# Other places for the results of the odd down projections, the mixer's weights kept as two parts, and GpSimd's tensor_tensor moved to VectorE

## The chip, the cores and the metric

The kernel runs on one core of one Trainium2 chip. The metric is the device time of one execution in microseconds (us); lower is better. Inputs and outputs lie in the chip's DRAM and are float32.

## What is computed

One layer of a streaming encoder on 2048 tokens of width 1024. The parts that matter here:

```python
mix = token_mixer(rms_norm(h, pre_mix_g), w_in, ..., w_out)   # p = xn @ w_in, mixing, y @ w_out
h = h + rms_norm(mix, post_mix_g)
f = rms_norm(h, pre_ffn_g) @ w_up                             # 1024 -> 2 x 2816
f = causal_dwconv3(f, ffn_conv_w) + ffn_conv_b
gate, up = split(f, 2)
ffn = (gelu(gate) * up) @ w_down                              # 2816 -> 1024
h = h + rms_norm(ffn, post_ffn_g)
```

The token mixer projects with `w_in`, has a gated short convolution over 512 channels and eight heads of a state recurrence (chunks of 64 tokens), and maps back with `w_out`.

## The kernel before

**Layout.** Channels lie on the 128 partitions, tokens along the free axis, in four token blocks of 512 (`TB`). Every matmul operand in full precision is split in two parts, a rounded higher part (`hi`, a copy on ScalarE) and the rest (`lo`, a subtraction on VectorE), and each product is three matmuls: hi x hi, hi x lo, lo x hi. `split` does this. In `gemm` weights come in blocks of four 128 x 128 tiles (256 KB): a DMA into `wraw`, the split into `whi` and `wlo`, then 12 matmuls. Each of the three rings has three buffers.

**Stages.** First the mixer runs over blocks 0 to 3. In block 0 the scale of the input norm comes late (`late`), so that projections are multiplied by it behind the matmul; `short_conv` does two such multiplications on GpSimd. The weights `w_in` of 26 column tiles are the same in every block: `gemm` with a name in `keep` stores the `lo` part in DRAM when a block is first used, and blocks 1 to 3 load the raw weights, copy `hi` on ScalarE, and load `lo`. In block 0 the second half of each tile's `lo` is computed on GpSimd. `out_proj(b)` does the output projection with `w_out`, eight column tiles of two weight blocks each, all split anew for every token block; `residual(b)` adds the input. `out_proj` and `residual` of a block run beside the mixer of the next.

Then the channel mixer. `up(0)` does the up projection for token blocks 0 and 1 together, then `down_block(0)` and `down_block(1)` the down projection, then `up(1)`, `down_block(2)` and `down_block(3)`. `up` runs over 22 column pairs; in each, seven products of 12 matmuls (a Strassen-like scheme for two token blocks and two halves of the columns) with weights a11, s1, s2, a12, s3, s4, a22 and the operands b11, t1, t2, b21, t3, b22, t4 in this order. `up(0)` computes the four sums s1 to s4 (`summed`; s1 and s3 on GpSimd, s2 and s4 on VectorE) and stores them; `up(1)` loads them. Behind the products come the convolution (`cv`), the gate (`gt`) and a store.

**Places.** `slot(n)` numbers SBUF places of 2 KB per partition: 0 to 39 and 56 to 78 in one pool, 40 to 55 in those of the mixer's operands. The operands of `up` occupy places 0 to 55 in the order of the products, four slices of two parts each, so that t4 takes 48 to 55. `down_block` keeps its 22 operands in other places, by turns (`places`), and its eight results `fo` in 48 to 55:

```python
fo = [slot(48 + d, f"fo{b}_{d}", F32) for d in range(KT)]
```

`down` accumulates 66 matmuls into one of two PSUM banks (`psD`); ScalarE squares it for the norm and copies it to `fo`. `finish` computes the norm's scale, spreads it over the partitions with `over_partitions` (`ps` in PSUM, `rb` its copy in SBUF), and for each of the eight tiles loads the residual into one of two buffers `ho`, multiplies `fo` by the scale, adds into `ho` and stores:

```python
if d < 3:
    pool_e.tensor_tensor(out=fd, in0=fd, in1=rb, op=ALU.mult)
else:
    dve.tensor_tensor(out=fd, in0=fd, in1=rps, op=ALU.mult)
(pool_e if d < 2 else dve).tensor_tensor(out=hk, in0=fd, in1=hk, op=ALU.add)
```

In the last block `finish` runs twice, on half the tokens each, with residuals loaded ahead (`held`). The raw operands of a down projection pass through the ring `gk` of three buffers.

**Order.** All operations are recorded in a `Plan` first. It computes an order by list scheduling, with costs for each engine and operation (`cost`), delays between engines, ranks (`R_CHAIN` before `R_EVAC`, `R_PREP`, `R_OPERAND`, `R_WEIGHT`, `R_GEMM`) in the first round and the latest starts in 15 more, and issues all engines' instructions in the best order found (`emit`, line 431, which is why every row of the profile names L431). There is one plan for the mixer and one for the rest. Every DMA is issued from SyncE's queue. An engine works off its instructions in the order issued.

## Time and profile before

| | |
|---|---|
| time before, median of 3 runs | 2590.94 us (2590.84 to 2595.94) |
| the profiled execution's own time | 2591.45 us |
| its span, first to last instruction | 2589.7 us |
| mean granted TensorE clock | 0.986 of full speed |
| busy: TensorE, VectorE, ScalarE, GpSimd | 2479.0, 2025.0, 1476.6, 152.8 us |
| DMA | 432.29 MB, mean 167 GB/s |

PE is TensorE, PEld its weight load, DVE is VectorE, ACT ScalarE, POOL GpSimd, SP SyncE. Rows of groups give the line, the engine, the operation, output <- inputs by tile name, the shape, the count, then the busy time in us and the mean duration of one in ns, then the engine's idle time before them and what ended it. Matmuls overlap, so that the mean of a matmul (some 390 ns) is longer than the distance between two.

### The profile page before, as it was taken

How to read it: one execution, taken by the hardware profiler on the slowest of the kernel's cores; microseconds unless marked ns; L12 is line 12 of the kernel's file. 1: busy time of each engine (PE TensorE's matmuls, PEld its weight loads, DVE VectorE, ACT ScalarE, POOL GpSimd, SP SyncE). 2: the span in 40 equal slices, each digit the busy share in tenths (PEclk: the TensorE clock that was granted, in tenths of full speed). 3: DMA queues.
4: the chain of work that ended last, by engine and by line, in shares of the span. 5: the costliest groups of instructions: out<-in, count | busy, mean ns of one | idle time of the engine just before them, and what ended most of it. 6: DMA issues, size and time to landing. Idle time of an engine off the chain costs nothing.

```text
span 2589.7 us, 41292 instructions
## 1 busy us (share of the span) xinstructions
PE 2479.0 (96%) x14210; PEld 1948.8 (75%) x14210; DVE 2025.0 (78%) x4159; ACT 1476.6 (57%) x3070; POOL 152.8 (6%) x116
## 2 busy tenths in 40 slices
PE   8988999999999899989999999999989999999997
PEld 6766777777786677667877778788868888888886
DVE  7989878889786889768999999855478787784534
ACT  7555766566656555456656566543456666673532
POOL 1311000000000000001111121001010000000001
PEclk9999999999999899989999999999999999999998
DMA  6535454557454675465464634775654444454653
GB/s 204 175 100 167 130 172 131 165 163 257 130 171 148 203 248 163 150 202 179 154 192 147 202 131 167 249 247 172 190 183 126 122 118 130 120 160 130 191 183 106
DMA packets 239970, 432.29 MB, mean 167 GB/s; under 512 B 26640, under 2 KB 33424, under 8 KB 239760
## 3 DMA queue, kind: packets, MB, share of 16 engines
q1 hardware_dynamic: 239760, 429.65, 52.7%
q8 instruction: 112, 1.84, 0.3%
q14 instruction: 98, 0.80, 0.1%
HBM read 321.54 MB, written 108.00 MB: 166 GB/s over the span
## 4 chain that ended last, share of the span: by engine, by line
PE 64%; DVE 20%; DMA 8%; issue 4%; ACT 4%; SPq 0%; POOL 0%; DVEq 0%; ACTq 0%; POOLq 0%
PE dn L431 17%; PE upa L431 13%; PE upc L431 6%; PE op L431 5%; PE upb L431 3%; PE rp_ps L431 3%; PE kp_ps L431 2%; PE pc L431 2%; DVE cv L431 2%; PE vp_ps L431 2%; PE ch_ps L431 2%; PE cb_ps L431 1%; PE cc_ps L431 1%; DVE gt L431 1%; PE y L431 1%
## 5 line engine op out<-in xcount | busy, mean ns | idle before, releaser
L431 DVE TENSOR_TENSOR wd_l<-wd_r,wd_h 128x512 fp32r<-128x512 f32 x198 | 129.9, 658 | 200.0 <-ACT wd_h L431 190.9
L431 DVE SCALAR_TENSOR_TENSOR cv<-co,vec,cv 128x512 f32<-128x512 f32 x352 | 272.9, 800 | 13.5 <-ACT cv L431 12.1
L431 PE MATMUL dn<-gh,wd_h 128*128 128x512 f32 (+1 forms) x726 | 281.2, 388 | 0.9 <-ACT gh L431 0.6
L431 PE MATMUL dn<-gh,wd_l 128*128 128x512 f32 (+1 forms) x726 | 280.1, 386 | 0.2 <-DVE wd_l L431 0.2
L431 PE MATMUL dn<-gl,wd_h 128*128 128x512 f32 (+1 forms) x726 | 279.0, 384 | 0.2 <-DVE gl L431 0.2
L431 ACT ACTIVATE wd_h<-wd_r 128x512 fp32r<-128x512 f32 x198 | 117.4, 595 | 251.7 <-PE dn L431 220.4
L431 DVE SCALAR_TENSOR_TENSOR gt<-gt,cv 128x512 f32<-128x512 f32 x264 | 177.5, 694 | 2.0 <-ACT gt L431 0.8
L431 ACT ACTIVATE cv<-co,vec 128x512 f32<-128x512 f32 x176 | 142.3, 811 | 44.2 <-DVE co L431 35.4
L431 PEld LDWEIGHTS dn<-gl,wd_h 128*128 128x128 f32 x726 | 136.3, 188 | 30.2 <-DVE gl L431 1.3
L431 PEld LDWEIGHTS dn<-gh,wd_l 128*128 128x128 f32 x726 | 136.4, 188 | 30.0 <-DVE wd_l L431 0.4
L431 PEld LDWEIGHTS dn<-gh,wd_h 128*128 128x128 f32 x726 | 136.4, 188 | 29.3 <-ACT gh L431 1.7
L431 ACT ACTIVATE wua_h<-wua 128x512 fp32r<-128x512 f32 x132 | 82.6, 626 | 82.1 <-issue 38.4
L431 PE MATMUL op<-y_h,wo_h 128*128 128x512 f32 x256 | 101.6, 406 | 5.3 <-ACT y_h L431 4.2
L431 PE MATMUL op<-y_l,wo_h 128*128 128x512 f32 x256 | 102.4, 404 | 0.6 <-DVE y_l L431 0.4
L431 PE MATMUL op<-y_h,wo_l 128*128 128x512 f32 x256 | 101.7, 402 | 0.2
L431 DVE TENSOR_TENSOR wua_l<-wua,wua_h 128x512 fp32r<-128x512 f32 x132 | 96.9, 735 | 4.8 <-ACT wua_h L431 4.7
L431 ACT ACTIVATE wus_h<-wus 128x512 fp32r<-128x512 f32 x88 | 55.6, 632 | 68.2 <-PE upa L431 25.2
L431 DVE TENSOR_TENSOR ut<-nt,um 128x120 f32<-128x120 f32 (+24 forms) x248 | 70.0, 282 | 5.4
L431 DVE TENSOR_TENSOR um<-um,ut 128x120 f32<-128x120 f32 (+24 forms) x248 | 70.1, 283 | 5.2
L431 POOL TENSOR_TENSOR fo<-fo,fn_rb 128x512 f32<-128x512 f32 (+1 forms) x15 | 17.7, 1197 | 941.9 <-ACT fn_rb L431 941.9
L431 DVE TENSOR_TENSOR gl<-gk,gh 128x512 fp32r<-128x512 f32 x88 | 59.0, 687 | 16.1 <-ACT gh L431 15.9
L431 ACT ACTIVATE gt<-cv 128x512 f32<-128x512 f32 x88 | 55.0, 625 | 25.4 <-DVE cv L431 24.6
(731 smaller groups left out, 7081.0 us busy)
## 6 DMA issues: line engine op xcount, KB each, us to landing
wd_r<-in_w_down SPq DMA_DIRECT2D x165, 256.0 KB, 2.8
wua<-in_w_up SPq DMA_DIRECT2D x154, 256.0 KB, 3.0
g_d<-gt SPq DMA_DIRECT2D x88, 256.0 KB, 2.6
gk<-g_d SPq DMA_DIRECT2D x88, 256.0 KB, 3.3
wus<-s_d SPq DMA_DIRECT2D x88, 256.0 KB, 3.2
wo_r<-in_w_out SPq DMA_DIRECT2D x64, 256.0 KB, 3.3
s_d<-wu1s SPq DMA_DIRECT2D x44, 256.0 KB, 3.1
x<-in_x_t SPq DMA_DIRECT2D x32, 256.0 KB, 4.2
```

Source lines behind the costliest of these rows:

```text
L431: getattr(getattr(self.nc, e), m)(*[real(a) for a in args], **{k: real(a) for k, a in kw.items()})
```

## The change

It has four parts. (1) `down_block` of odd blocks (1 and 3) keeps its results 0 to 4 in places 51 to 55 and 5 to 7 in the ring `gk`; even blocks as before. (2) `gemm` with `keep` stores both parts of a weight block at its first use and loads both parts afterwards, without raw weights and without a split; `out_proj` uses it too. (3) Every tensor_tensor of GpSimd becomes VectorE's: the lower parts of kept weights in block 0, the late scale in `short_conv`, the sums s1 and s3, and the multiplications and additions of `finish`. (4) `finish` takes the scale from PSUM alone, and the copy `rb` falls away there. Since a plan orders everything, the order of all engines is computed anew.

```diff
--- before.py
+++ after.py
@@ -485,7 +485,13 @@
         act(hi, src, AF.Copy)
         lo_engine.tensor_tensor(out=lo, in0=src, in1=hi.bitcast(F32), op=ALU.subtract)
 
-    lower = {}
+    parts_d = {}
+
+    def store_parts(hi, lo, name):
+        there = [dram.tile([128, 4, 128], F32, name=f"{name}{p}") for p in "hl"]
+        for part, t in zip((hi, lo), there):
+            nc.sync.dma_start(out=t, in_=part.bitcast(F32))
+        return there
 
     def gemm(ps, src, nk, xs, name, keep=None, early=False):
 
@@ -495,19 +501,18 @@
         for k0 in range(0, nk, 4):
             n = min(4, nk - k0)
             plan.rank = R_PREP if early else R_WEIGHT
-            raw = wst.tile([128, 4, 128], F32, tag="wraw", name=f"{name}_r{k0}", bufs=WB[0])
-            nc.sync.dma_start(out=raw[:, 0:n, :], in_=src[:, k0:k0 + n, :])
             hi = wst.tile([128, 4, 128], F32R, tag="whi", name=f"{name}_h{k0}", bufs=WB[1])
             lo = wst.tile([128, 4, 128], F32R, tag="wlo", name=f"{name}_l{k0}", bufs=WB[1])
-            if (keep, k0) in lower:
-                act(hi, raw, AF.Copy)
-                nc.sync.dma_start(out=lo.bitcast(F32), in_=lower[keep, k0])
+            kept = parts_d.get((keep, k0))
+            if kept:
+                for part, there in zip((hi, lo), kept):
+                    nc.sync.dma_start(out=part.bitcast(F32), in_=there)
             else:
-                split(raw[:, 0:n, :], hi[:, 0:n, :], lo[:, 0:n, :],
-                      pool_e if keep and k0 else dve)
+                raw = wst.tile([128, 4, 128], F32, tag="wraw", name=f"{name}_r{k0}", bufs=WB[0])
+                nc.sync.dma_start(out=raw[:, 0:n, :], in_=src[:, k0:k0 + n, :])
+                split(raw[:, 0:n, :], hi[:, 0:n, :], lo[:, 0:n, :], dve)
                 if keep:
-                    lower[keep, k0] = dram.tile([128, 4, 128], F32, name=f"{keep}_l{k0}")
-                    nc.sync.dma_start(out=lower[keep, k0], in_=lo.bitcast(F32))
+                    parts_d[keep, k0] = store_parts(hi, lo, f"{keep}_{k0}")
             plan.rank = R_GEMM
             for k in range(n):
                 wh, wl = hi[:, k, :], lo[:, k, :]
@@ -541,7 +546,8 @@
                           op0=ALU.mult, op1=ALU.add)
         rsqrt(o1, ms, [128, n], name, out=out)
 
-    def over_partitions(y, name, pool, tag, bufs=1, both=False, n=4):
+    def over_partitions(y, name, pool, tag, bufs=1, n=4):
+
 
         dg = o1.tile([128, 4, 128], F32, tag="sq", name=f"{name}_dg")
         ps = psN.tile([128, TB], F32, tag="g", name=f"{name}_ps")
@@ -552,10 +558,12 @@
             for s in range(n):
                 nc.tensor.matmul(ps[:, s * 128:(s + 1) * 128], ones, dg[:, s, :],
                                  start=True, stop=True)
+        ps = ps[:, 0:n * 128]
+        if pool is None:
+            return ps
         rb = pool.tile([128, TB], F32, tag=tag, name=f"{name}_rb", bufs=bufs)[:, 0:n * 128]
-        ps = ps[:, 0:n * 128]
         act(rb, ps, AF.Copy)
-        return (rb, ps) if both else rb
+        return rb
 
     def token_sums(accs, name, n=4):
 
@@ -605,7 +613,7 @@
         acc = new_acc(f"oacc{b}")
         for d in range(KT):
             ps = psA.tile([128, TB], F32, tag="a", name=f"op{b}_{d}")
-            gemm(ps, w_out[d], KT, xs, f"wo{b}_{d}")
+            gemm(ps, w_out[d], KT, xs, f"wo{b}_{d}", f"wo{d}")
             ov = o1.tile([128, TB], F32, tag="ov", name=f"ov{b}_{d}", bufs=2)
             act(ov, ps, AF.Copy)
             nc.sync.dma_start(out=mix_d[b][:, d, :], in_=ov)
@@ -1159,8 +1167,8 @@
                 ps = proj(16 + 3 * j, f"cb{nm}")
                 dve.tensor_tensor(out=u[:, 2:TB + 2], in0=ps, in1=u[:, 2:TB + 2], op=ALU.mult)
                 if late is not None:
-                    pool_e.tensor_tensor(out=u[:, 2:TB + 2], in0=u[:, 2:TB + 2], in1=late,
-                                         op=ALU.mult)
+                    dve.tensor_tensor(out=u[:, 2:TB + 2], in0=u[:, 2:TB + 2], in1=late,
+                                      op=ALU.mult)
                 act(ucar[:, j, :], u[:, TB:TB + 2], AF.Copy)
                 cv = m1.tile([128, TB], F32, tag="cv", name=f"cv{nm}", bufs=1)
                 act(cv, u[:, 2:TB + 2], AF.Copy, scale=v_("conv_a", 8 + j))
@@ -1171,7 +1179,7 @@
                 ps = proj(17 + 3 * j, f"cc{nm}")
                 dve.tensor_tensor(out=cv, in0=ps, in1=cv, op=ALU.mult)
                 if late is not None:
-                    pool_e.tensor_tensor(out=cv, in0=cv, in1=late, op=ALU.mult)
+                    dve.tensor_tensor(out=cv, in0=cv, in1=late, op=ALU.mult)
                 nc.sync.dma_start(out=y_d[b][:, j, :], in_=cv)
 
             def first_operand():
@@ -1339,11 +1347,11 @@
                 split(raw, hi, lo, dve)
                 return hi, lo
 
-            def summed(a, b, op, j, engine, o=None):
+            def summed(a, b, op, j, o=None):
                 plan.rank = R_WEIGHT
                 if o is None:
                     o = next_slot(SUM, 2, f"wu{j}s{nm}", F32, (128, 4, 128))
-                engine.tensor_tensor(out=o, in0=a, in1=b, op=op)
+                dve.tensor_tensor(out=o, in0=a, in1=b, op=op)
                 nc.sync.dma_start(out=s_d[i][:, j, :, :], in_=o)
                 return o
 
@@ -1353,14 +1361,14 @@
                 a11, a12, a21, a22 = (load(x, n) for x, n in ((ga, "a11"), (gb, "a12"),
                                                               (ua, "a21"), (ub, "a22")))
                 yield parts(a11, "a11")
-                s1 = summed(a21, a22, ALU.add, 0, pool_e)
+                s1 = summed(a21, a22, ALU.add, 0)
                 yield parts(s1, "s1")
-                s2 = summed(s1, a11, ALU.subtract, 1, dve)
+                s2 = summed(s1, a11, ALU.subtract, 1)
                 yield parts(s2, "s2")
                 yield parts(a12, "a12")
-                s3 = summed(a11, a21, ALU.subtract, 2, pool_e)
+                s3 = summed(a11, a21, ALU.subtract, 2)
                 yield parts(s3, "s3")
-                s4 = summed(a12, s2, ALU.subtract, 3, dve, s2)
+                s4 = summed(a12, s2, ALU.subtract, 3, s2)
                 yield parts(s4, "s4")
                 yield parts(a22, "a22")
             else:
@@ -1485,7 +1493,9 @@
             if beside:
                 beside()
             plan.rank = R_EVAC
-            fo = [slot(48 + d, f"fo{b}_{d}", F32) for d in range(KT)]
+
+            fo = [f1.tile([128, TB], F32, tag="gk", name=f"fo{b}_{d}", bufs=3) if d > 4 and b % 2
+                  else slot((51 if b % 2 else 48) + d, f"fo{b}_{d}", F32) for d in range(KT)]
             acc = new_acc(f"facc{b}")
 
             def down(d, t, apart=False):
@@ -1504,19 +1514,16 @@
                 n = (t.stop - t.start) // 128
                 rf = f1.tile([128, 4], F32, tag="rf", name=f"rf{nm}")[:, 0:n]
                 inv_rms(token_sums(accs, nm, n), nm, rf, n)
-                rb, rps = over_partitions(rf, nm, o1, "nrb", both=True, n=n)
+                rps = over_partitions(rf, nm, None, "nrb", n=n)
                 for d in range(KT):
                     if last:
                         hk = held[d][:, t]
                     else:
-                        hk = f1.tile([128, TB], F32, tag="ho", name=f"ho{b}_{d}", bufs=2)
-                        nc.sync.dma_start(out=hk, in_=h_d[b][:, d, :])
+                        hk = f1.tile([128, TB], F32, tag="ho", name=f"ho{nm}_{d}", bufs=2)[:, t]
+                        nc.sync.dma_start(out=hk, in_=h_d[b][:, d, t])
                     fd = fo[d][:, t]
-                    if d < 3:
-                        pool_e.tensor_tensor(out=fd, in0=fd, in1=rb, op=ALU.mult)
-                    else:
-                        dve.tensor_tensor(out=fd, in0=fd, in1=rps, op=ALU.mult)
-                    (pool_e if d < 2 else dve).tensor_tensor(out=hk, in0=fd, in1=hk, op=ALU.add)
+                    dve.tensor_tensor(out=fd, in0=fd, in1=rps, op=ALU.mult)
+                    dve.tensor_tensor(out=hk, in0=fd, in1=hk, op=ALU.add)
                     nc.sync.dma_start(out=out_t[:, b, d, t], in_=hk)
 
             tokens = slice(0, TB)
@@ -1524,9 +1531,9 @@
                 down(d, tokens)
             if last:
 
-                held = [slot(d, f"ho{b}_{d}", F32) for d in range(KT)]
-                for d in range(KT):
-                    nc.sync.dma_start(out=held[d], in_=h_d[b][:, d, :])
+                held = [slot(d, f"ho{b}_{d}", F32) for d in range(KT if last else 0)]
+                for d, hk in enumerate(held):
+                    nc.sync.dma_start(out=hk, in_=h_d[b][:, d, :])
                 for t in (slice(0, TB // 2), slice(TB // 2, TB)):
                     plan.rank = R_EVAC
                     finish(t, [down(KT - 1, t, True), acc[:, t]])
```

## Rows read from the trace of the kernel before

**Rows 1.** Busy time by stretch: bounds, length, then each engine (x instructions), granted clock, DMA.
```profile
0.00:260.00 260.00, 227.03 (x1464) 171.32 (x1465) 230.29 (x504) 154.51 (x343) 49.82 (x46) 0.97 0.50 162
260.00:1180.00 920.00, 886.52 (x6751) 670.80 (x6750) 739.54 (x1956) 557.18 (x1264) 3.07 (x3) 0.98 0.55 175
1180.00:1626.00 446.00, 431.56 (x1865) 345.84 (x1864) 424.20 (x664) 278.71 (x567) 69.59 (x42) 0.99 0.50 166
...
1880.00:1936.00 56.00, 44.01 (x178) 32.13 (x177) 43.71 (x76) 28.69 (x53) 8.09 (x5) 0.91 0.61 195
1936.00:2323.00 387.00, 387.00 (x1690) 316.84 (x1689) 315.07 (x491) 246.14 (x472) 0.00 (x0) 1.00 0.45 128
2323.00:2590.00 267.00, 250.54 (x1166) 206.63 (x1164) 127.98 (x237) 100.64 (x178) 15.28 (x15) 0.97 0.51 154
sum 2590.00, PE 2479.01 PEld 1948.77 DVE 2025.03 ACT 1476.63 POOL 152.80; mean PE 354.14 PEld 278.40 DVE 289.29 ACT 210.95 POOL 21.83
```

**Rows 2.** The chain that ended last, longest pieces: start us, length us, what.
```profile
1649.07 110.16 PE dn L431 x479
...
1935.82 5.48 PE upa L431 x24
...
2301.38 5.56 PE upa L431 x24
```

**Rows 3.** Timeline of TensorE, second up pass: start, length, engine, [idle before <- releaser].
```profile
1880.62 0.39 PE L431 MATMUL upa<-b_10h,wua_h 128*128 128x512 f32 x1
...
1916.53 0.50 PE L431 MATMUL upa<-t_12h,wua_h 128*128 128x512 f32 x1 [3.35 <-ACT t_12h L431]
...
1923.09 0.80 PE L431 MATMUL upa<-t_13h,wua_h 128*128 128x512 f32 x1 [3.44 <-ACT t_13h L431]
```

**Rows 4.** Timeline of VectorE, GpSimd and ScalarE in the same step.
```profile
1891.33 0.68 DVE L431 TENSOR_TENSOR fo<-fo,fn_ps 128x512 f32<-128x512 f32 x1
...
1897.97 1.77 DVE L431 TENSOR_TENSOR b_13l<-xrb,b_13h 128x512 fp32r<-128x512 f32 x1
...
1908.20 1.32 DVE L431 TENSOR_TENSOR ho<-fo,ho 128x512 f32<-128x512 f32 x2
...
1921.68 1.40 DVE L431 TENSOR_TENSOR ho<-fo,ho 128x512 f32<-128x512 f32 x2 [3.30 <-DMA ho<-h_d]
...
1895.76 3.43 POOL L431 TENSOR_TENSOR ho<-fo,ho 128x512 f32<-128x512 f32 x2
...
1922.41 0.63 ACT L431 ACTIVATE t_13h<-xrt 128x512 fp32r<-128x512 f32 x1 [5.93 <-DVE ho L431]
```

**Rows 5.** Timeline of VectorE, from the first to the second down projection.
```profile
1779.80 0.69 DVE L431 TENSOR_TENSOR ho<-fo,ho 128x512 f32<-128x512 f32 x1 [0.80 <-DMA ho<-h_d]
```

**Rows 6.** Groups of VectorE in the first up pass, 1180 to 1620 us.
```profile
L431 DVE SCALAR_TENSOR_TENSOR cv<-co,vec,cv 128x512 f32<-128x512 f32 x166 | 139.0, 859 | 4.1 <-ACT cv L431 3.4
...
L431 DVE TENSOR_TENSOR wua_l<-wua,wua_h 128x512 fp32r<-128x512 f32 x64 | 50.0, 782 | 1.6 <-ACT wua_h L431 1.6
...
L431 DVE TENSOR_TENSOR wu1s<-wu0s,wua 128x512 f32<-128x512 f32 x21 | 14.3, 682 | 3.8 <-POOL wu0s L431 3.8
```

**Rows 7.** Groups of VectorE in the second up pass, 1940 to 2330 us.
```profile
L431 DVE SCALAR_TENSOR_TENSOR cv<-co,vec,cv 128x512 f32<-128x512 f32 x160 | 115.0, 748 | 8.3 <-ACT cv L431 7.6
...
L431 DVE TENSOR_TENSOR wua_l<-wua,wua_h 128x512 fp32r<-128x512 f32 x59 | 40.3, 684 | 0.0
```

**Rows 8.** Groups of ScalarE over the whole span.
```profile
L431 ACT ACTIVATE wo_h<-wo_r 128x512 fp32r<-128x512 f32 x64 | 39.8, 627 | 39.1 <-PE op L431 24.9 <-DMA wo_r<-in_w_out 6.6 <-DVE td L431 2.1
```

**Rows 9.** What TensorE waited for: us in total, times, longest us.
```profile
PE vp_ps L431 <- DMA vp_l<-wi_l: 1.3, 2, 0.8
```

**Rows 10.** Timeline of VectorE at the end of the last block.
```profile
2580.32 0.42 DVE L431 TENSOR_TENSOR fo<-fo,fn_ps 128x256 f32<-128x256 f32 x1 [1.18 <-PE fn_ps L431]
2581.27 0.42 DVE L431 TENSOR_TENSOR fo<-fo,fn_ps 128x256 f32<-128x256 f32 x1 [0.53 <-ACT fn_rb L431]
...
2584.63 1.63 DVE L431 TENSOR_TENSOR ho<-fo,ho 128x256 f32<-128x256 f32 x3
```

## The prediction

> **What bounds the kernel now.** I read the table of stretches first, one line per stage [rows 1]. TensorE is busy 2479 of 2590 us, so all that other engines can give back is some 111 us of its idle time, and the question of each edit is where in those it lies. The stages are the mixer of token block 0 (33.0 us idle), the mixers of blocks 1 to 3 with the output projection (33.5), the first pass of the up projection (14.4), the step from the second down projection into the second up pass (12.0 of 56) and the end of the last down projection (16.5 in the last line). Two stages run close to VectorE: 424.2 of 446 us in the first up pass, 230.3 of 260 in block 0. In the second up pass, without GpSimd, VectorE has 315 of 387 us and TensorE never waits. GpSimd works 152.8 us in all, 49.8 in block 0 and 69.6 in the first up pass.
>
> Then the chain that ended last, for the second up pass [rows 2]: the runs of 24 matmuls (last product of one column pair, first of the next) come every (2301.38 - 1935.82)/19 = 19.24 us. They are the last 20 of the 21 joins of 22 pairs, so the first joins pairs 1 and 2. The pass begins at 1880.62 [rows 3]. Unhindered, this join would start one pair and six of seven products later: 19.24 + 16.49 = 35.7 us, at 1916.4. It starts at 1935.82: 19.4 us lost, some 2 of them to the 16 small matmuls of the norm between. Of the other 17, 12.0 are idle [rows 1]; the rest are matmuls at the lower of the clock's two levels (granted 0.91 on average there against 1.00 later).
>
> Last, the timeline at that step. The long waits of TensorE are for the operand t4 [rows 3], which is written to places 48 to 55, and those hold the results `fo` of block 1 until `finish` has used them. VectorE's adds of `ho` come in pairs, results 2 and 3 at 1908.20, 6 and 7 at 1921.68, 4 and 5 between, because only two `ho` buffers exist: each pair waits for two stores and then two loads (3.30 us before the last) [rows 4]. ScalarE's split of t4's last slice starts 5.93 us late behind them.
>
> **Part 1, the places of the results.** For odd blocks `fo` 0 to 4 go to places 51 to 55 and 5 to 7 into the `gk` buffers. Places 48 to 50 are then free for t4 from the start, and its last place, 55, needs only `fo` 4, not `fo` 7. When? Now the first two results go through GpSimd, whose adds end at 1895.76 + 3.43 = 1899.2. On VectorE the same four operations are 4 x 0.69 = 2.8 us from about 1891.4, when its first `fo` product started: over at 1894.2, 5.0 us sooner. A round of stores and loads takes 6.7 us ((1921.68 - 1908.20)/2) [rows 4]. So `fo` 2 and 3 fall due near 1903 and `fo` 4 near 1910, and the last slice of t4 can be split at about 1911 in place of 1922.4: 12 us earlier. Bounds: 17 if products of pair 1 fill what is left (two of them, 5.5 us, are not tied to t4); 5 if VectorE, which here also splits the new operands, falls behind, since it gets five more operations there (3.4 us) and queues the t4 splits behind them. GpSimd also blocks VectorE here: one operand split took 1.77 us [rows 4] against 0.68 to 0.70 usually, and that goes. I take 12.
>
> The other side of the move is the next block's first result, which must wait for `fo` 3 of the block before it instead of `fo` 0 (blocks 0 to 1, 2 to 3). In block 0 the add of `fo` 3 stands at 1779.80 [rows 5]; the matmuls of block 0 end at 1649.07 + 110.16 = 1759.2 [rows 2], 21 us earlier. A down product is 66 matmuls at 5.48/24 us, 15.1 us, and there are two PSUM banks, so TensorE needs the first drained only after 30 us: 9 us of cover. Cost 0; if the round grew past the cover, each us would be one of TensorE, at most some 5.
>
> **Part 2, GpSimd's work on VectorE, first up pass.** 44 sums s1 and s3 move: GpSimd takes 69.59/42 = 1.66 us for one [rows 1], VectorE 0.682 for the same shape [rows 6]: +30.0 us on an engine 95% busy. Against this stands what GpSimd's running costs VectorE. The same operations in the two passes: `cv` 0.859 against 0.748 us, 166 times, 18.4 us; the weight split `wua_l` 0.782 against 0.684, 64 times, 6.3 us [rows 6, 7]. Also 3.8 us in which VectorE waited for s1 [rows 6]. Sum: 30.0 - 24.7 - 3.8 = +1.5 us, nothing on a stage of 446. I take 0; bounds +8 (the waits come back elsewhere) and -15 (below).
>
> On this the Trainium skill (SBUF — State Buffer, section Who interferes with whom) says that a VectorE instruction with two SBUF inputs and a GpSimd instruction that reads SBUF lock each other out for the whole instruction, whoever comes second. The 1.77 us split agrees. By the rule alone each sum could cost VectorE a whole GpSimd operation, 44 x 1.66 = 73 us, against the 24.7 of the rows; by it the stage would fall to TensorE's pace, and the total to the time of the second rival.
>
> **Block 0.** 34 operations move (26 lower parts of weights, 8 products with the late scale): 34 x 0.684 = +23.3 us. Relief at the rate of the up pass, 24.7 per 69.6 us of GpSimd, is 17.7 on 49.8.  Net +5.6 on VectorE; the stage is bound by it only in parts, so I take +2, bounds -5 and +6.
>
> **Part 3, weights kept as parts.** Blocks 1 to 3 load both parts instead of raw and lower: for w_in as many loads, 156 ScalarE splits fewer; for w_out (48 blocks of 64) one load more each, one ScalarE and one VectorE split fewer. 204 x 0.627 [rows 8] = 128 us off ScalarE's 557 and 48 x 0.684 = 33 us off VectorE's 740 in that stage [rows 1]. Little of it is on the path: TensorE idles 33.5 us in 920. New: the higher part is loaded into a ring of three, and its transfer can begin only when an earlier block is done. The lower parts live with this today: a block is 12 matmuls, 2.7 us, so two blocks of cover, 5.5 us, and TensorE waited 1.3 us in all for the `vp` ones [rows 9]. SP's queue gets as many issues for w_in, the lower part behind the higher by one issue; 16 more loads per projection, and 68 stores more in blocks 0 and 1 (52 higher parts of w_in, 16 of w_out) plus 16 of w_out's lower parts, with DMA at 0.50 to 0.55 busy [rows 1]. Bounds: -10 (a third of the idle time) to +8 (204 loads, each 0.04 us late). I take -2.
>
> **Part 4, the end.** From 2580.32 VectorE and GpSimd share 16 operations on 256 columns, until 2584.63 + 1.63 = 2586.26 [rows 10]: 5.9 us. VectorE alone has at most 16 x 0.42 = 6.7 us, less where neighbours overlap, and does not wait 0.53 us for the copied scale. I take 0, bounds -1 and +1. The copies of the scale (three 512 wide, two 256 wide) leave ScalarE, which was idle or off the path there.
>
> **Sum.** -12 + 0 + 2 - 2 + 0 = -12 us. The profiled execution took 2591.45 us (span 2589.7); that gives 2579.4. The median of the runs shown is 0.5 us below it: 2579.
>
> **Rivals.**
> Second: the lock between the engines costs more than the durations show (waits of ScalarE for VectorE behind it), and the first up pass falls to TensorE's pace. 22 x 19.24 = 423 us against 446, less some 2 for the norms' matmuls: up to 20, of which 15 would be got. 2579 - 15 = 2564. For it: VectorE at 95%. Against: it loses only 24.7 us by the rows and gets 30 new.
>
> Third, the other side: VectorE becomes the bound of both its stages. If only half of the relief comes (the slow `cv` may come from something else than GpSimd), then 12.3 us in the first up pass and 8.9 in block 0 go on the path: 2579 + 21 = 2600. It decides from some 17 us of the 42.4 on: 2579 + 17 is 2596, 0.2% above the median. Against: GpSimd is the one difference between `cv` in the two passes that I see.
>
> Fourth: the step into the second up pass does not close, because the round trips of `ho` or the queue of VectorE hold t4 up: the gain there is 4 instead of 12, 2587, no change by the bound below. For it: only two `ho` buffers, as now.
>
> Fifth: the kept parts arrive late in the projections, +8 in place of -2: 2589, no change.
>
> **How the numbers follow.** My forecast 0.50, second 0.10, third 0.14, fourth 0.15, fifth 0.11. What a measurement of this kernel can tell from no change is 0.2%, 5.2 us: faster is below 2585.8, slower above 2596.1. Faster: 0.47 of the first, 0.10 of the second, 0.10 of the fourth and fifth (they lie near the line), 0.03 of the third: 0.70. Slower: 0.10 of the third, 0.03 of the fifth: 0.13. Same: the rest, 0.17. The range goes from 2563 (just past the second) to 2594 (the third's nearer part); the forecast's own is 2574 to 2586, from the bounds 17 and 5 of the first term.
>
> **What the profile of the changed kernel would show.** Part 1: the first regular run of 24 matmuls starts some 43 us after the pass begins, not 55, and t4's last split some 12 us sooner against the pass's start. Part 2: `cv` in the first up pass at 0.75 us, VectorE's busy time there within 8 us of 424, the stage within 8 us of 446. Part 3: ScalarE down by some 130 us, TensorE's waits for DMA'd parts below 8 us. The prediction is wrong if `cv` stays at 0.86, if t4 still waits for `ho` loads for 8 us and more, or if the order of the plan, which is computed anew, opens waits in a stage that the edits don't touch.

## The result, and the profile after

The changed kernel took 2535.97 us (median of 4 runs, 2530.97 to 2538.9) against 2593.44 of the kernel before (4 runs): ratio 0.9775, interval 0.9752 to 0.9799. That is 57.5 us less, where the prediction had 12 and its range ended at 2563. The profiled execution has a span of 2531.6 us, 58.1 less than before's 2589.7, so the two traces show the whole difference. TensorE does the same 14210 matmuls in both. Of the 58.1 us, 44.7 are idle time of TensorE and 13.4 its busy time (2479.0 to 2465.6 us): a wait also costs something in the matmuls behind it, as the first up pass shows below.

The table of stretches of the changed kernel, in the order of [rows 1]: block 0's 260 us, the rest of the mixer, the first up pass, the down projections 0 and 1, the step, the second up pass, the end.

```profile
0.00:260.00 260.00, 239.50 (x1506) 183.45 (x1507) 230.19 (x554) 154.83 (x345) 2.06 (x12) 0.97 0.64 220
260.00:1160.23 900.23, 872.22 (x6704) 660.24 (x6703) 707.84 (x1892) 446.44 (x1056) 0.17 (x1) 0.99 0.61 199
1160.23:1588.90 428.67, 427.89 (x1885) 349.84 (x1884) 417.46 (x708) 287.48 (x572) 0.00 (x0) 1.00 0.53 174
1588.90:1839.04 250.14, 249.34 (x1094) 202.87 (x1093) 146.26 (x244) 108.39 (x195) 0.00 (x0) 1.00 0.69 217
1839.04:1895.00 55.96, 53.46 (x236) 42.21 (x235) 53.37 (x98) 36.83 (x70) 0.00 (x0) 1.00 0.69 211
1895.00:2270.00 375.00, 375.00 (x1638) 307.25 (x1637) 305.37 (x476) 238.58 (x458) 0.00 (x0) 1.00 0.46 131
2270.00:2531.60 261.60, 248.21 (x1157) 205.04 (x1155) 126.98 (x248) 97.22 (x171) 0.00 (x0) 0.98 0.51 155
sum 2531.60, PE 2465.62 PEld 1950.89 DVE 1987.47 ACT 1369.76 POOL 2.23; mean PE 352.23 PEld 278.70 DVE 283.92 ACT 195.68 POOL 0.32
```

Read two columns first. In the first up pass (third line) TensorE now idles 0.8 us and VectorE 11.2, where the same pass of the kernel before, cut at the same operations, reads:

```profile
1178.78:1630.28 451.50, 437.06 (x1892) 350.45 (x1891) 427.73 (x668) 283.00 (x576) 70.50 (x43) 0.99 0.50 166
```

So VectorE executes 40 more instructions (708 against 668) in 10.3 us less busy time. And in the first 260 us TensorE does 239.5 us of work instead of 227.0 [rows 1], while VectorE is as busy as before with 50 instructions more.

With both traces cut at the same operations (first matmul of the first up pass, first of the down projection, first and last of the second up pass; in the mixer ScalarE's first read of the projection `wa_ps` in blocks 1 and 3), the 58.1 us lie as follows:

| stretch | before | after | change | forecast |
|---|---|---|---|---|
| block 0 of the mixer | 255.3 | 245.2 | -10.1 | +2 (part 2) |
| blocks 1 and 2 | 563.3 | 566.4 | +3.1 | -2 (part 3), for this line and the next |
| block 3 and last output projection | 360.2 | 348.6 | -11.6 | |
| first up pass | 451.5 | 428.7 | -22.8 | 0 (part 2) |
| down projections 0 and 1 | 250.3 | 250.1 | -0.2 | 0 |
| second up pass, with the step (first to last start) | 442.8 | 429.3 | -13.5 | -12 (part 1) |
| down projections 2 and 3, end | 266.3 | 263.2 | -3.1 | 0 (part 4) |

A line of the table comes from one execution of each kernel. Block 0, which is the same program in the changed kernel and in `f1` and `f2` below, read 245.2, 240.6 and 247.1, so it moves by some 3 us to either side; the other lines of the mixer, the same program there too, by some 2 us in all (566.4, 568.5, 568.4 and 348.7, 350.1, 350.3).

**The step.** Two of the later joins in the chain that ended last, and TensorE's timeline at the step:

```profile
1919.44 5.48 PE upa L431 x24
...
2246.52 5.56 PE upa L431 x24
```

```profile
1839.04 0.39 PE L431 MATMUL upa<-b_10h,wua_h 128*128 128x512 f32 x1
...
1861.19 0.50 PE L431 MATMUL upa<-t_12h,wua_h 128*128 128x512 f32 x1 [0.17 <-ACT t_12h L431]
...
1869.50 0.50 PE L431 MATMUL upa<-t_13l,wua_h 128*128 128x512 f32 x1 [0.61 <-DVE t_13l L431]
```

The joins of 19.24 us, counted back from the last as in [rows 2], put the first at 2246.52 - 19 x 19.24 = 1880.96 (where the chain has it), 41.9 us behind the start of the pass; it was 55.2 [rows 2, 3], and the prediction said 43. The waits of 3.35 and 3.44 us for t4 [rows 3] are 0.17 and 0.61, and TensorE idles 2.5 us in the 56 of the step instead of 12.0 [rows 1]. What ends them is still the chain of `ho`: t4's last slice goes to places 54 and 55, and its two parts are split behind VectorE's sums for `fo` 3 and `fo` 4. VectorE and ScalarE there:

```profile
1861.84 0.69 DVE L431 TENSOR_TENSOR hofn<-fo,hofn 128x512 f32<-128x512 f32 x1
...
1867.50 0.68 DVE L431 TENSOR_TENSOR hofn<-fo,hofn 128x512 f32<-128x512 f32 x1
...
1868.76 0.68 DVE L431 TENSOR_TENSOR t_13l<-xrt,t_13h 128x512 fp32r<-128x512 f32 x1
```

```profile
1862.56 0.63 ACT L431 ACTIVATE t_13h<-xrt 128x512 fp32r<-128x512 f32 x1 [1.42 <-DVE hofn L431]
```

The higher part is split 23.5 us after the pass began, where it had taken 1922.41 - 1880.62 = 41.8 [rows 3, 4]. The lower part, the last split of t4, comes 29.7 us after it, where the kernel before has 42.6:

```profile
1923.18 0.69 DVE L431 TENSOR_TENSOR t_13l<-xrt,t_13h 128x512 fp32r<-128x512 f32 x1
```

That is 12.9 us sooner; the prediction said some 12.

**The first up pass.** Groups of VectorE in it (1160 to 1590 us), those of [rows 6]:

```profile
L431 DVE SCALAR_TENSOR_TENSOR cv<-co,vec,cv 128x512 f32<-128x512 f32 x168 | 121.7, 744 | 1.3 <-ACT cv L431 1.2
...
L431 DVE TENSOR_TENSOR wua_l<-wua,wua_h 128x512 fp32r<-128x512 f32 x64 | 43.7, 683 | 0.0
...
L431 DVE TENSOR_TENSOR wu1s<-wu0s,wua 128x512 f32<-128x512 f32 x21 | 14.3, 683 | 0.0
```

`cv` fell from 859 to 744 ns and `wua_l` from 782 to 683, to the durations of the second pass [rows 7]. What TensorE waited for in the pass before the change (total us, times, longest; the four largest of seven lines):

```profile
PE upa L431 <- ACT m L431: 6.0, 6, 3.4
PE hn_tsum L431 <- DVE hacc L431: 2.9, 1, 2.9
PE upa L431 <- DVE co L431: 2.3, 4, 0.8
PE upa L431 <- ACT u L431: 1.6, 2, 0.9
```

and after it, the only line left:

```profile
PE upa L431 <- DVE co L431: 0.7, 1, 0.7
```

`m`, `u` and `co` are the drains of products into SBUF and the sums on them, `hacc` the sum of squares for a norm: TensorE had mostly stood behind VectorE's and ScalarE's work on results, and 0.8 us in all behind a weight.

The two longest waits lead back to a load and not to an instruction that GpSimd held up; what made the load late was not followed further. In the wait of 3.4 us ScalarE's copy `m` at 1451.19 stood behind its square of the residual, which had waited for VectorE, and VectorE for a load:

```profile
1447.94 0.75 DVE L431 SCALAR_TENSOR_TENSOR md<-md,vec,on_rb 128x512 f32<-128x512 f32 x1 [2.10 <-DMA md<-mix_d]
```

```profile
1450.05 0.63 ACT L431 ACTIVATE h_sq<-md 128x512 f32<-128x512 f32 x1 [4.65 <-DVE md L431]
1450.65 0.63 ACT L431 ACTIVATE gt<-cv 128x512 f32<-128x512 f32 x1
1451.19 0.58 ACT L431 ACTIVATE m<-upa 128x512 f32<-128x512 f32 x1
```

Ahead of the wait of 2.9 us VectorE had waited 1.08 us for the same kind of load. Behind each of the two waits TensorE ran at the lower of its clock's two levels for 3.4 us (the last three numbers of a line are granted clock, DMA share, GB/s):

```profile
1340.60:1344.00 3.40, 3.40 (x12) 2.82 (x11) 3.40 (x5) 1.67 (x4) 2.32 (x1) 0.50 0.20 77
1453.20:1456.60 3.40, 3.40 (x10) 2.62 (x9) 2.33 (x5) 2.19 (x7) 0.00 (x0) 0.50 0.79 208
```

So the 22.8 us of this pass are 13.6 us of TensorE's idle time (14.4 to 0.8) and 9.2 us of its busy time (437.1 to 427.9). By an estimate from these rows, 3.4 of the 9.2 are the 6.8 us at half the clock; the rest was not followed. After the change the granted clock is 1.00 throughout the pass.

### The profile page after: what moved, and what is told of

It reads as the page before. It is cut to its first block, busy times and chain, and to the rows that moved or that the text cites. A ratio compares the mean times of both kernels' runs of the same rounds, so it can differ in the third digit from the quotient of the medians.

```text
span 2531.6 us, 41036 instructions
## 1 busy us (share of the span) xinstructions
PE 2465.6 (97%) x14210; PEld 1950.9 (77%) x14210; DVE 1987.5 (79%) x4214; ACT 1369.8 (54%) x2861; POOL 2.2 (0%) x13
## 4 chain that ended last, share of the span: by engine, by line
PE 78%; DVE 12%; DMA 6%; issue 2%; ACT 2%; SPq 0%; DVEq 0%; POOLq 0%; ACTq 0%
PE dn L431 18%; PE upa L431 18%; PE upc L431 9%; PE op L431 6%; PE upb L431 4%; PE vp_ps L431 3%; PE kp_ps L431 3%; PE pc L431 2%; PE rp_ps L431 2%; PE cc_ps L431 2%; PE ch_ps L431 2%; PE cb_ps L431 2%; PE y L431 1%; DMA x<-in_x_t 1%; DVE armk L431 1%
## 5 line engine op out<-in xcount | busy, mean ns | idle before, releaser
L431 PE MATMUL dn<-gh,wd_h 128*128 128x512 f32 (+1 forms) x726 | 281.0, 388 | 0.3 <-ACT gh L431 0.3
L431 PE MATMUL dn<-gh,wd_l 128*128 128x512 f32 (+1 forms) x726 | 279.6, 386 | 0.2 <-DVE wd_l L431 0.2
L431 DVE TENSOR_TENSOR wd_l<-wd_r,wd_h 128x512 fp32r<-128x512 f32 x198 | 127.4, 645 | 193.5 <-ACT wd_h L431 184.7
L431 PE MATMUL dn<-gl,wd_h 128*128 128x512 f32 (+1 forms) x726 | 278.5, 384 | 0.6 <-DVE gl L431 0.6
L431 DVE SCALAR_TENSOR_TENSOR cv<-co,vec,cv 128x512 f32<-128x512 f32 x352 | 253.9, 745 | 9.3 <-ACT cv L431 8.4
L431 ACT ACTIVATE wd_h<-wd_r 128x512 fp32r<-128x512 f32 x198 | 117.6, 594 | 248.3 <-PE dn L431 208.9
L431 DVE SCALAR_TENSOR_TENSOR gt<-gt,cv 128x512 f32<-128x512 f32 x264 | 174.7, 684 | 0.6
L431 PEld LDWEIGHTS dn<-gh,wd_l 128*128 128x128 f32 x726 | 136.4, 188 | 30.7 <-DVE wd_l L431 1.1
L431 PEld LDWEIGHTS dn<-gl,wd_h 128*128 128x128 f32 x726 | 136.4, 188 | 30.2 <-DVE gl L431 1.3
L431 PEld LDWEIGHTS dn<-gh,wd_h 128*128 128x128 f32 x726 | 136.4, 188 | 28.8 <-ACT wd_h L431 1.0
L431 ACT ACTIVATE cv<-co,vec 128x512 f32<-128x512 f32 x176 | 141.3, 811 | 26.0 <-DVE co L431 18.5
L431 ACT ACTIVATE wua_h<-wua 128x512 fp32r<-128x512 f32 x132 | 82.8, 628 | 81.5 <-issue 43.5
L431 PE MATMUL op<-y_h,wo_h 128*128 128x512 f32 x256 | 103.9, 412 | 9.5 <-ACT y_h L431 4.9
L431 PE MATMUL op<-y_h,wo_l 128*128 128x512 f32 x256 | 103.6, 409 | 1.4 <-DMA wo_l<-wo_0l 1.3
L431 PE MATMUL op<-y_l,wo_h 128*128 128x512 f32 x256 | 102.1, 405 | 0.1
L431 DVE TENSOR_TENSOR wua_l<-wua,wua_h 128x512 fp32r<-128x512 f32 x132 | 90.1, 683 | 3.0 <-ACT wua_h L431 2.9
L431 ACT ACTIVATE wus_h<-wus 128x512 fp32r<-128x512 f32 x88 | 55.6, 631 | 64.1 <-ACT cv L431 22.7
L431 ACT ACTIVATE sv<-sn,pct 64x64 f32<-64x64 f32 x112 | 32.5, 336 | 79.4 <-DVE sn L431 78.9
L431 DVE TENSOR_TENSOR um<-um,ut 128x120 f32<-128x120 f32 (+24 forms) x248 | 66.7, 269 | 5.6
L431 ACT ACTIVATE gh<-gk 128x512 fp32r<-128x512 f32 x88 | 54.9, 626 | 28.5 <-DMA gk<-g_d 26.0
L431 DVE TENSOR_TENSOR ut<-nt,um 128x120 f32<-128x120 f32 (+24 forms) x248 | 64.7, 261 | 5.4
L431 DVE TENSOR_TENSOR gl<-gk,gh 128x512 fp32r<-128x512 f32 x88 | 59.3, 687 | 11.6 <-ACT gh L431 11.2
```

The source lines that it names most:

```text
L431: getattr(getattr(self.nc, e), m)(*[real(a) for a in args], **{k: real(a) for k, a in kw.items()})
```

## The experiments

Fifteen kernels ran, each against the kernel before on the same chip. Ratios with their intervals, and the lengths of the stages in one profiled execution (us; "up 1", "down" and "rest" are the first up pass, the down projections 0 and 1, and all behind):

| kernel | ratio | interval | mixer | up 1 | down | rest |
|---|---|---|---|---|---|---|
| before | 1 | | 1178.8 | 451.5 | 250.3 | 709.1 |
| after | 0.9775 | 0.9752-0.9799 | 1160.2 | 428.7 | 250.1 | 692.6 |
| e1_swap_only | 0.9926 | 0.9905-0.9947 | 1181.2 | 440.9 | 250.0 | 708.9 |
| e2_vectore_only | 0.9867 | 0.9848-0.9887 | 1175.6 | 430.5 | 249.1 | 705.6 |
| e3_places_only | 0.9968 | 0.9957-0.9980 | 1181.7 | 453.6 | 251.3 | 702.9 |
| e4_parts_only | 1.0015 | 1.0003-1.0026 | 1181.3 | 454.3 | 248.8 | 710.0 |
| f1_reads_beside | 0.9833 | 0.9816-0.9850 | 1159.3 | 444.2 | 251.0 | 696.1 |
| f2_writes_beside | 0.9779 | 0.9757-0.9800 | 1165.8 | 429.2 | 250.0 | 693.7 |
| f3_back_on_gpsimd | 0.9836 | 0.9818-0.9855 | 1174.9 | 435.9 | 251.9 | 692.8 |
| f4_w_out_split | 0.9774 | 0.9751-0.9798 | 1162.5 | 429.5 | 250.6 | 692.1 |
| g1_changed_other_order | 0.9762 | 0.9747-0.9776 | 1161.4 | 429.8 | 248.7 | 694.0 |
| g2_before_other_order | 0.9968 | 0.9955-0.9981 | 1175.7 | 451.0 | 249.2 | 709.6 |
| g3_vectore_other_order | 0.9847 | 0.9830-0.9863 | 1171.5 | 429.4 | 248.3 | 705.1 |
| g4_parts_other_order | 1.0022 | 1.0012-1.0031 | 1189.9 | 452.8 | 249.3 | 708.9 |
| h1_parts_swap | 0.9950 | 0.9931-0.9969 | 1177.8 | 444.0 | 249.8 | 709.7 |
| h3_places_vectore | 0.9832 | 0.9812-0.9852 | 1176.5 | 429.5 | 250.4 | 695.6 |
| i1_true_price | 1.0010 | 0.9999-1.0022 | 1182.4 | 452.1 | 245.9 | 712.1 |

**One part at a time.** `e1` keeps the order of before to the last instruction and issues GpSimd's arithmetic on VectorE, in `emit`:

```diff
+                if e == "gpsimd" and ops[i][1] == "tensor_tensor":
+                    e = "vector"
```

> Every tensor_tensor of GpSimd is issued on VectorE, at the place in the order that the plan of the kernel before gave it; nothing else differs, and nothing is planned anew. Theory A (GpSimd's reads of SBUF hold VectorE up, and more than its longer instructions show): most of the gain of the first up pass and of block 0 is here without a new order, 20 to 35 us faster, cv in the first up pass at 0.75 us. Theory B (the new order is what helps; the engine alone does not): 0 to 30 us slower, since VectorE gets 30 us in the first up pass and 23 in block 0 at places chosen for another engine.

`e2` moves the same operations in the source (`pool_e` to `dve`), so that the order is planned anew; `finish` multiplies by `rps` throughout.

> GpSimd's tensor_tensor moved to VectorE and planned anew; places and weights as before. Theories A and B: the stretch from the first up product to the second up pass 23 us shorter (as in the changed kernel), block 0 some 10 us shorter, 33 to 38 us in all. Theory C (the kept parts are what shortens the mixer and unloads ScalarE): under 25 us.

`e3` takes only the new `fo`, `e4` only the kept parts (the lower parts of the second halves stay on GpSimd).

> Only the places of the odd blocks' results. All theories: the second up pass starts regularly 12 to 14 us earlier after its first product, nothing else: 10 to 15 us faster. If the step also needed GpSimd's work gone: under 8.

> Only the weights of the mixer and the output projection kept as two parts (GpSimd still computes the second half of the first lower parts of w_in). Theories A and B: 4 to 10 us faster, all behind block 0 in the mixer. Theory C: 15 us or more. If late transfers eat it: 0, with TensorE waiting over 8 us for transfers of parts.

The first up pass belongs to the move from GpSimd: it is 10.6 us shorter with the old order (`e1`) and 21.0 with one planned for it (`e2`); places and parts alone leave it at 454. In `e1` `cv` is at 746 ns already, as theory A expected, and the whole is some 19 us faster, just short of its 20 to 35. The places alone give 6 us in the second up pass (436.8 against 442.8), the move alone 2 (440.8). The parts alone cost some 4 us, where 4 to 10 us of gain were expected. The medians of the three parts alone sum to -1.33 - 0.32 + 0.15 = -1.5%, and the whole is -2.25%: some 20 us come from their meeting.

**Does GpSimd hold VectorE up, and by what?** Three kernels put work back on GpSimd beside the changed kernel. `f1` issues, behind each of the 44 sums s1 and s3, three operations on GpSimd that read the sum and write a scratch tile which nobody reads; `f2` one of a single column, which orders it behind the sum, and six memsets of the scratch tile, which only write; `f3` issues the moved operations (the sums, and the 34 of block 0) on GpSimd again, in the order of the changed kernel.

The main lines (`...` marks what is left out); `beside` names the sums s1 and s3, `f` is the sum, `s` the scratch tile, `pooled` names the moved operations:

```diff
 f1
+                if i in self.beside:
+                    ...
+                    for lo, hi in ((0, 192), (192, 384), (384, 512)):
+                        g.tensor_tensor(out=s[:, 0:hi - lo], in0=f[:, lo:hi], in1=f[:, lo:hi],
+                                        op=ALU.mult)
 f2
+                if i in self.beside:
+                    ...
+                    g.tensor_tensor(out=s[:, 0:1], in0=f[:, 0:1], in1=f[:, 0:1], op=ALU.mult)
+                    for _ in range(6):
+                        g.memset(s[:], 0.0)
 f3
+                e = "gpsimd" if i in self.pooled else ops[i][0]
```

> The changed kernel with work for GpSimd that nothing waits for: behind each of the 44 sums s1 and s3 of the first up pass, which stay on VectorE, GpSimd multiplies the sum by itself, 512 columns in three instructions, into a spare place (two SBUF inputs). Order of all else as in the changed kernel. Theory A (reads of GpSimd hold VectorE up): the first up pass 15 to 30 us longer than its 428.7, cv there near 0.85 us. Theory B (only order and queueing matter): within 3 us of the changed kernel, cv at 0.75.

> As the one before, but GpSimd reads one column of the sum and then fills the spare place six times with zeros: busy as long, nearly without reads. Theory A: within 4 us of the changed kernel. If GpSimd's mere work beside VectorE costs (any access, not reads): 15 us longer as with reads.

> The order planned for the changed kernel, with the 34 moved operations of block 0 and the 44 sums issued on GpSimd again (finish stays on VectorE). Theory A: the first up pass 15 to 25 us longer, block 0 8 to 12 us longer, blocks 1 to 3 unchanged in length. Theory B: the order keeps its gain, under 8 us longer in all.

The first up pass of `f1`, as a stretch, and then groups of VectorE and of GpSimd in it (1160 to 1590 us, so that some of the last operations are not counted):

```profile
1159.27:1603.50 444.23, 434.59 (x1886) 347.12 (x1885) 438.77 (x706) 283.70 (x571) 123.43 (x129) 1.00 0.51 167
```

```profile
L433 DVE SCALAR_TENSOR_TENSOR cv<-co,vec,cv 128x512 f32<-128x512 f32 x164 | 125.7, 785 | 1.3 <-ACT cv L433 1.1
...
L433 DVE TENSOR_TENSOR wus_l<-wu0s,wus_h 128x512 fp32r<-128x512 f32 x21 | 16.5, 784 | 0.0
```

```profile
L440 POOL TENSOR_TENSOR scratch<-wu2s 128x192 f32<-128x192 f32 x42 | 57.0, 1356 | 169.1 <-DVE wu2s L433 167.5
L440 POOL TENSOR_TENSOR scratch<-wu0s 128x192 f32<-128x192 f32 x42 | 31.1, 741 | 182.5 <-DVE wu0s L433 180.8
```

(L433 is the changed kernel's L431: these files are two lines longer ahead of it.) The pass of `f2`, in the same three views:

```profile
1165.85:1595.05 429.20, 427.77 (x1886) 349.81 (x1885) 417.45 (x707) 287.31 (x572) 101.28 (x301) 1.00 0.52 173
```

```profile
L433 DVE SCALAR_TENSOR_TENSOR cv<-co,vec,cv 128x512 f32<-128x512 f32 x166 | 120.5, 746 | 1.3 <-ACT cv L433 1.2
```

```profile
L441 POOL MEMSET scratch<- 128x192 f32 x258 | 66.9, 259 | 14.9
L439 POOL TENSOR_TENSOR scratch<-wu2s 128x1 f32<-128x1 f32 x22 | 25.2, 1144 | 168.7 <-DVE wu2s L433 168.7
L439 POOL TENSOR_TENSOR scratch<-wu0s 128x1 f32<-128x1 f32 x21 | 9.2, 438 | 179.9 <-DVE wu0s L433 179.9
```

With 706 instructions in place of 708, VectorE is busy 438.8 us instead of 417.5 when GpSimd reads beside it, and the pass takes 15.6 us longer, though no engine waits for GpSimd in the pass. `cv` rises only to 785 ns, less than expected: the lengthening is spread over the operations that follow a sum. In `f2` GpSimd is busy 101 us (123 in `f1`), 67 of them in memsets and the rest in reads of one column, and nothing moves (417.5, +0.5). So it is the reading of whole tiles, not GpSimd's being busy. The operations `co<-upa,m` of VectorE, whose first input lies in PSUM, fit with this: they take 682 ns on average before, 678 in `f1` and 685 after. GpSimd pays too: the same operation on 128x192 takes 741 or 1356 ns by where it falls among VectorE's. `f3` makes the pass 7.2 us longer than after, about half of what was expected, with `cv` at 847 ns and VectorE busy 5.6 us longer with 43 instructions fewer, and block 0 is at 254.7 again, as expected.

The Trainium skill (SBUF — State Buffer, Who interferes with whom) says that a VectorE instruction with two SBUF inputs contends with a GpSimd instruction that reads SBUF, and not with one that only writes. `f1` and `f2` agree, with 15.6 and 0.5 us.

**Is it the order?** The first up passes of `e1` and `e2` differ by 10.4 us, with the same operations on VectorE in another order. `STAY` weighs how strongly the planner keeps TensorE on one kind of matmul; 9 in place of 10 gives every kernel another order of the mixer, and another order of VectorE and ScalarE in the first up pass to `g1` and `g3`. In `g2` the traces show that pass in the order of the kernel before.

```diff
-STAY = 10.0
+STAY = 9.0
```

> The changed kernel with the plan's weight on staying with one kind of matmul (STAY) at 9 instead of 10: the same instructions in another order. Theory A (the gains belong to the instructions): first up pass and step as in the changed kernel within 4 us, the mixer within 6 us. Theory B (they belong to one lucky order): 15 us or more given back.

> The kernel before with STAY 9. Theory A: within 10 us of it, the first up pass still 445 us or more. Theory B: another order alone gains 15 us or more.

> Only the operations moved to VectorE, STAY 9. If the mixer's 13 us between this version (1175.6) and the changed kernel's family (1160 to 1166) belong to the kept parts: again 1172 or more. If to the order: anywhere from 1160 to 1180.

> Only the kept parts, STAY 9. If kept parts help the mixer only once GpSimd's reads are gone: the mixer again 1178 or more. If the +12 us in blocks 1 and 2 of the first such run were that order's: 1165 to 1175.

Without GpSimd the first up pass stays at 429.4 (`g3`) and 429.8 (`g1`). With GpSimd, `g2` says nothing of another order there, but `e4`, `g4` and `i1` below have one, and take 454.3, 452.8 and 452.1. So it is no luck of one order. The mixer moves by 1 to 9 us with the order, which is what one order is worth there.

What the orders planned with GpSimd have in common shows in TensorE's clock: in the first up pass of before, `e1`, `e3`, `e4`, `g2`, `g4`, `h1` and `i1` it is at the lower level for 3.4 to 10.2 us, and in no kernel whose order was planned without GpSimd. In `e1` it is 6.8 us, behind a wait of 2.3 us for the norm's sum; with the idle time (7.1 us against 1.9) that is most of the 10.4 us to `e2`.

`i1` tells the planner what the trace showed, a GpSimd `tensor_tensor` of 1660 ns where it reckons with 1223:

```diff
-        base, each = {"tensor_tensor": (148, 2.1), ...
+        base, each = {"tensor_tensor": (150, 2.95), ...
```

> The kernel before, unchanged but for one number of its planner: the price of a GpSimd tensor_tensor of 128x512 is 1660 ns, as the trace showed in the first up pass, in place of 1223. Swapping the engine in the old order gave 10.6 us in the first up pass, and the order planned anew with the sums on VectorE gave 10.4 more. Theory: that second half comes from the planner's picture of GpSimd, which is too short by 0.44 us an operation, so that products were placed as if the sums were ready; then this order gets a good part of it, 5 to 10 us of the 451.5 of that pass (ratio about 0.997). Rival: what the picture lacks is the time that VectorE loses to GpSimd, which no price of GpSimd tells it; then the pass stays at 451 within 3 us, and the ratio is 0.999 to 1.002.

The pass takes 452.1 us: the theory of the wrong price fell. What the planner lacks is not GpSimd's time. It may be VectorE's loss, which no price of the planner holds; no run here shows that.

**The parts and the move together.** `h1` is `e4` with the two lines of `e1`; `h3` is `e2` with the lines of `e3`: the changed kernel without its kept parts, but with the copies `rb` of the scale still made on ScalarE (five in the whole run, for which VectorE waits 3.0 us). `f4` is the changed kernel with `w_out` split anew each time, as before:

```diff
-gemm(ps, w_out[d], KT, xs, f"wo{b}_{d}", f"wo{d}")
+gemm(ps, w_out[d], KT, xs, f"wo{b}_{d}")
```

> The order planned for kept parts with GpSimd, and every tensor_tensor of GpSimd issued on VectorE in that order. If the order is what costs 12 us in blocks 1 and 2: that stretch (563 us before, 575 with the parts alone, 566 to 569 in the changed kernel) stays at 572 or more, and only block 0 (3 to 10 us) and the first up pass (some 11 us) get shorter. If GpSimd's use in block 0 delays the later blocks: 566 to 569.

> Places and moved operations, w_in and w_out as before. If the step needs both and not the parts: the second up pass 429 to 431 us long against 442.8 before, 436.8 with the places alone and 440.8 with the moved operations alone; the mixer 1171 to 1176; in all 46 to 50 us faster than before.

> The changed kernel with w_out split anew in every block, as before; w_in kept as two parts. If w_out's splits off VectorE and ScalarE are what shortens the mixer's end (block 3 and the last output projection): some 10 us longer there, 8 to 14 us in all. If it is w_in's: within 3 us of the changed kernel.

Places and move add up: `h3` has 0.9832, the two alone 0.9968 and 0.9867. The parts are what does not add: they cost 4 us alone, and from `h3` to after, which differ by them and by the five copies, the ratio goes from 0.9832 to 0.9775, some 15 us. The mixer's stretches show where (blocks 1 and 2, then block 3 with the last output projection). `e4`, and `e2` for the orders without parts:

```profile
258.10:833.50 575.40, 562.04 (x4492) 425.74 (x4491) 453.06 (x1252) 294.44 (x705) 0.00 (x0) 0.99 0.56 184
833.50:1181.30 347.80, 324.94 (x2263) 244.04 (x2263) 259.90 (x668) 157.41 (x363) 1.46 (x2) 0.98 0.67 220
```

```profile
247.90:811.70 563.80, 555.80 (x4411) 422.50 (x4409) 458.38 (x1254) 354.61 (x817) 0.00 (x0) 0.99 0.52 165
811.70:1175.57 363.87, 336.24 (x2354) 254.36 (x2351) 286.84 (x724) 203.57 (x455) 0.17 (x1) 0.95 0.59 188
```

The last stretch is 348 to 354 us in most kernels with parts, 358 in `f4` and 356 in `g4`, and 360 to 365 in those without: the gain is there with either engine. But in the orders planned with GpSimd in the mixer, blocks 1 and 2 give it back: 575.4 (`e4`), 576.6 (`g4`), and 572.2 in `h1`, where GpSimd does nothing any more. After has 566.4. So most of the loss belongs to the order planned beside GpSimd's work and not to GpSimd at work (`h1` is one execution, 3 us below `e4`, about the scatter); why that order is worse stays open. `w_out`'s parts are worth nothing net (`f4` 0.9774). They shorten the end from 358.1 to 348.6 us, as expected, while blocks 1 and 2 go from 563.9 to 566.4, and block 0 differs by 4.6, within its scatter.

## Why the prediction was wrong

**Part 2, first up pass: the step that failed.** "Sum: 30.0 - 24.7 - 3.8 = +1.5 us, nothing on a stage of 446. I take 0". It measured -22.8. Two things were wrong in it.

First, the relief was too small. VectorE took on 42 sums in the pass as cut, 28.8 us, and its busy time fell by 10.3: some 39 us went, not 24.7. The durations of its instructions account for 32.5 of them. The prediction had counted only the two groups with the largest means, `cv` (19.0) and `wua_l` (6.3); `gt` (700 to 683 ns, some 120 times), the residual's operations and the short ones of the norms were held up as well. The other 6.6 us are records of neighbouring instructions that overlap more (54 us in place of 47).

Second, and more, a stage was valued by the busy time of an engine that was 95% busy. VectorE idled 23.8 of the 451.5 us, and TensorE lost time in waits for `m`, `co`, `u` and the norm's sum, and in the slower clock behind the longest of them. After the change VectorE runs 417.5 of 428.7 us, as full as 97%, and TensorE does not wait: 22 x 19.24 = 423 plus the norms. The prediction's own signs say the same: `cv` came to 744 ns for 0.75 us, and VectorE's busy time within 8 us of 424, but the stage did not come within 8 us of 446.

Of the 23 us, 7 to 11 are the engine in a given order (`f3`, `e1`); the rest needs an order planned for VectorE (`e2`, `g3`, `h3`). The two longest waits of the kernel before lead back to loads of the residual, and why the orders planned with GpSimd meet them stays open. The second rival had this pass fall to TensorE's pace and got 0.10; the pass did so, and GpSimd's reads are part of the reason (`f1`, `f2`). GpSimd's whole time in the pass, 70.5 us, was not lost: VectorE's busy time shows 39.

**Block 0.** "Net +5.6 on VectorE [...] so I take +2". It measured -10.1, with a scatter of some 3; it is the same sum at the same wrong rate. `f3`, 254.7 against 240.6 to 247.1 in the same order, says that it is the engine. In the order of before the engine gave only 2.7 us there (`e1`, 252.6), which is within the scatter.

**Part 3.** "I take -2". It measured -8.5 over blocks 1 to 3, or some -15 by the ratios of `h3` and after, past the bound of -10, and +4 with the parts alone. The bounds held the late transfers, and these cost little, as said: TensorE's waits for kept parts in blocks 1 and 2 are 2.4 us. What was missing is that the order decides whether TensorE gets anything of the work saved on the other engines. ScalarE's busy time fell by 107 us, not 130; 209 instructions went (3070 to 2861: the 204 counted and the copies of the scale), at 0.51 us each in place of 0.627.

**Part 1.** This was right: -13.5 for -12, the first join 41.9 us into the pass for 43, t4's last split 12.9 us sooner for 12. But the whole does not come from the places: they give 6 alone, the move 2, and both without the parts 11.1 (431.7, `h3`). The prediction had both in the term, the ends of GpSimd's adds and its blocked splits among them.

**Part 4.** The forecast was 0 with bounds of 1 us; the stretch measured -3.1. This is hardly scatter: it takes 264.8 to 267.0 us in the kernels whose order was planned with `finish` on GpSimd, and 262.4 to 264.8 in the others. From the last matmul of a down projection to the end it is 15.3 us in place of 17.4, of which the prediction saw one part: the 16 operations at the very end took 5.4 us for 5.9 [rows 10].

```profile
2523.27 0.75 DVE L431 TENSOR_TENSOR fo<-fo,fn_ps 128x256 f32<-128x256 f32 x2 [1.18 <-PE fn_ps L431]
...
2527.94 0.75 DVE L431 TENSOR_TENSOR ho<-fo,ho 128x256 f32<-128x256 f32 x2
```

Ahead of them TensorE's last wait, for the norm's `fn_dg`, fell from 4.9 to 3.6 us; the prediction had left the norm out.

**The rivals.** The third, VectorE as the bound, fell: at 97% it cost TensorE 0.8 us of idle time. The fourth and fifth fell with parts 1 and 3. No kernel here is faster than the changed one beyond the intervals; `g1` (0.9762) and `f4` overlap it.

## What to carry to other kernels

Work on a second engine is not free because that engine has time: compare the same operation's mean duration with and without it beside, over all groups, and take the sum of the lengthenings as the least that the move gives back (32.5 of 39 us here). A stage whose two engines are both at some 95% or more is valued by who waits for whom, not by the busy sum: ask what the stage would take at TensorE's pace, and whether the other engine's work fits in it. Count a long wait of TensorE with the slower clock behind it. And judge an edit that feeds a planner in the order that it will have, since the same parts cost 4 us in an order planned with GpSimd and gave some 15 in one planned without it.

## What the runs showed of the hardware

GpSimd operations of one column in `f2` took 1144 ns on average behind one sum and 438 behind the other, and the time goes by what VectorE does meanwhile. Seven of the 43 took 194 or 195 ns, each while VectorE worked on `co`, whose first input lies in PSUM. All others met operations with both inputs in SBUF and took 507 ns or more, up to 4.18 us where several of those stood in a row. One of each kind, with what VectorE did:

```profile
1199.96 0.19 POOL L439 TENSOR_TENSOR scratch<-wu0s 128x1 f32<-128x1 f32 x1 [8.26 <-DVE wu0s L433]
1206.78 0.57 POOL L439 TENSOR_TENSOR scratch<-wu2s 128x1 f32<-128x1 f32 x1 [4.71 <-DVE wu2s L433]
```

```profile
1199.73 0.69 DVE L433 TENSOR_TENSOR co<-upb,m 128x512 f32<-128x512 f32 x1
...
1206.55 1.41 DVE L433 SCALAR_TENSOR_TENSOR cv<-co,vec,cv 128x512 f32<-128x512 f32 x2
```

VectorE's operations on 4 columns are held up too: `hn_t` took 337 ns in `f3` and 153 after. TensorE's granted clock fell to 0.50 for 3.4 us behind idle times of 2.9 and 3.4 us in the kernel before. And VectorE at 97% of a stretch let TensorE run at its full pace, busy 427.9 of 428.7 us.
